# Weight operands of the MLP's first two pairs of chunks: made during the in-projection and loaded later

## The chip, the cores and the metric

The kernel runs on one core of a Trainium2 chip. The metric is the device time of one execution in microseconds (us); the kernel before takes 1713.9 us, the median of three executions (1712.73 to 1714.35). Engines: PE is TensorE (PEld its weight loads), DVE is VectorE, ACT is ScalarE, POOL is GpSimd, and SP is the engine whose queue issues nearly all transfers.

## The reference

One encoder layer over two groups of tokens (1024 and 256, together 1280) of width 1024, in fp32, with the same weights. Cut to what matters here:

```python
n = _rms_norm(h, g_mix, NORM_EPS)
z = jnp.einsum('bsd,dc->bsc', n, w_in).astype(f32)        # in-projection, 2304 columns
qa, ka, va, qb, kb, vb = jnp.split(z, cuts, axis=-1)
# mixer A: differential attention, 4 heads; mixer B: grouped-query attention with rotary positions
mixed = jnp.concatenate([oa, ob], axis=-1).astype(h.dtype)
h = h + jnp.einsum('bsc,cd->bsd', mixed, w_out)            # out-projection
n2 = _rms_norm(h, g_mlp, NORM_EPS)
a = jax.nn.relu(jnp.einsum('bsd,df->bsf', n2, w_ff1))      # MLP, 4096 columns
h = h + jnp.einsum('bsf,fd->bsd', a * a, w_ff2)
# then a gated per-layer embedding, and a final RMSNorm of h
```

The gain `g_mlp` of the norm is a factor on the rows of `w_ff1`. It depends on inputs alone, and so do all operands that are made from `w_ff1`; the products with them need `n2`, which is there only after the attention and the out-projection.

## The kernel before

**Numbers.** Every fp32 operand is split into a high part (type fp32r, by a copy on ScalarE) and a low part (operand minus high part, on VectorE or POOL). A product is three matmuls: high by high, high by low and low by high.

**Stages, by the trace.** In-projection to about 190 us; attention from then to about 720 us, with the rest of the in-projection and the out-projection woven in; a transition at 700 to 800 us, in which the last rows of the out-projection, the second norm, the transposes of the normed rows and the first products of the MLP run beside each other; first MLP product to about 1164 us; second to about 1530 us; then the gate, the embedding and the final norm.

**In-projection.** The pieces `b_unit` (queries, keys and values of mixer B, with norm and rotary positions), `va_unit` (values of mixer A) and `qk_a` (queries and keys of mixer A) are Python generators that yield after some matmuls. `weave` draws from two of them in turn. A tile of `b_unit` or `va_unit` is 24 matmuls of 128 x 256 into one PSUM bank (`psb`, `psv`, two banks each), which ScalarE (L283, L367) and then VectorE (L284, L368) read. Weights come by `load_w`: raw halves (`rawp`, `rawa`) are loaded, copied by ScalarE (L175) and subtracted (L176). `load` chains transfers of inputs: each is issued after the one before it in program order.

**First MLP product.** The 4096 columns are 32 chunks of 128, taken as 16 pairs (`NP1`). A pair is one step of a Strassen-Winograd scheme: 7 products instead of 8, each of a sum of quarters of the activations by a sum of quarters of the weights, in the order `O1` = 1, 6, 7, 2, 5, 4, 3. For each pair `w1_load` loads two raw blocks of 512 KB and multiplies them by the gain on POOL (eight pieces, L1012). `w1_ops` makes four sums (L1093, L1094, L1103, L1104) and seven splits (high L1087 on ScalarE, low L1088). For pairs 0 and 1 (`GS`) sums and all splits' low parts are on VectorE, for later pairs the sums and two of the low parts on POOL. The operands live in slots `W0` to `W11`; four of these, in rotation, take raw blocks. The activations' operands are split in `n_split` (high `nhi` L1120, low `nlo` L1121), from sums (`mlp_sums`, L1056) of transposed blocks (`trn`, copied by ScalarE in L1032 to `nb`); some pieces of them wait in `nlo` after a transfer that POOL issues (L1039). The first pair's products are made in two parts, 384 and then 256 columns of tokens, since the last two rows are normed last.

**What sets the order.** Each engine runs its own list of instructions in order. The lists are set when the kernel is built, by a scheduler that respects dependences and the orders that the program writes out (`issue_after`, `behind_norm`). In the transition the loop over `side` decides after how many finished rows of the out-projection (`op_done`) the loads of raw blocks and the first split are placed.

## Time and profile before

| what | value |
|---|---|
| median of three executions | 1713.9 us (1712.73 to 1714.35) |
| profiled execution: its time | 1711.62 us |
| profiled execution: its span | 1709.8 us |
| mean granted clock of TensorE | 0.997 |
| PE busy | 1668.8 us, 98% of the span |
| VectorE busy | 1183.8 us, 69% |
| ScalarE busy | 862.6 us, 50% |
| POOL busy | 686.2 us, 40% |

The span goes from the first to the last instruction of the profiled execution; the difference to its own time lies around it. The profile has a page with busy times per engine and per group of instructions, and the trace behind it gives the waits of an engine with what ended them, the timeline, and busy time by stretch with the clock that TensorE was granted.

### The profile page before, as it was taken

The numbers are of one execution on the slowest core, as the hardware profiler recorded it, in microseconds if no ns is written. First come the engines' busy times: TensorE is split into PE (matmuls) and PEld (weight loads), VectorE is DVE, ScalarE is ACT, GpSimd is POOL, SyncE is SP. The second block draws the span as 40 slices with busy tenths as digits, with TensorE's granted clock in tenths as the row PEclk, the third lists the DMA queues.
The fourth block names the chain that finished last, engine by engine and source line by source line (L and its number), as shares of the span: only waits on it lengthen the run. The fifth ranks groups of instructions, "written<-read, shape, count | busy, mean of one in ns | idle before, by whom it ended". The sixth has DMA issues, their size and how long they took to land.

```text
span 1709.8 us, 27198 instructions
## 1 busy us (share of the span) xinstructions
PE 1668.8 (98%) x9849; PEld 1488.8 (87%) x9849; DVE 1183.8 (69%) x2115; ACT 862.6 (50%) x1733; POOL 686.2 (40%) x667
## 2 busy tenths in 40 slices
PE   8999999999999999989999999999999999999997
PEld 8999889888788888879999999998888888888886
DVE  7866588787888878589775666666554865445666
ACT  8522377677766667684333333333333333354644
POOL 1224455555743444536565655520533400001441
PEclk9999999999999999999999999999999999999999
DMA  9923764433953623472443344359666465532111
GB/s 316 267 91 114 202 170 124 139 90 104 268 161 112 168 81 111 149 221 104 158 150 123 125 154 134 130 201 362 205 218 203 125 201 189 171 119 70 42 44 50
DMA packets 187835, 263.60 MB, mean 154 GB/s; under 512 B 13226, under 2 KB 120628, under 8 KB 187700
## 3 DMA queue, kind: packets, MB, share of 16 engines
q1 hardware_dynamic: 185956, 256.60, 47.4%
q0 software_dynamic: 1600, 5.24, 1.0%
q8 instruction: 78, 1.28, 0.3%
q14 instruction: 57, 0.47, 0.1%
q10 hardware_dynamic: 144, 0.00, 0.0%
HBM read 175.29 MB, written 81.27 MB: 150 GB/s over the span
## 4 chain that ended last, share of the span: by engine, by line
PE 76%; DVE 9%; ACT 4%; issue 4%; DMA 3%; POOL 3%; SPq 1%; POOLq 0%; DVEq 0%; ACTq 0%
PE psa L240 6%; PE sc L573 6%; PE av L651 5%; PE tr L627 4%; PE pso L240 4%; PE psb L240 3%; PE psv L240 2%; PE psg L1497 2%; DVE pl L638 1%; DVE nlo L1121 1%; DMA xt<-in_x 1%; DMA xr<-in_xT 1%; PE f__16240 L156 1%; PE f__15200 L156 1%; PE f__16582 L156 1%
## 5 line engine op out<-in xcount | busy, mean ns | idle before, releaser
L1299 ACT ACTIVATE ao<-ar 128x1280 fp32r<-128x1280 f32 x56 | 71.3, 1275 | 193.4 <-PE f__16244 L156 37.9
L573 PE MATMUL sc<-kt,qt 128*128 128x512 f32 (+1 forms) x576 | 156.7, 392 | 7.6 <-ACT p L598 4.8
L638 DVE TENSOR_TENSOR pl<-tr,ph 128x512 fp32r<-128x512 f32 x204 | 137.9, 684 | 31.2 <-ACT ph L633 29.9
L1301 DVE TENSOR_TENSOR ao<-ar,ao 128x1280 fp32r<-128x1280 f32 x56 | 88.8, 1587 | 100.1 <-ACT ao L1299 100.1
L633 ACT ACTIVATE ph<-tr 128x512 fp32r<-128x512 f32 x204 | 119.8, 595 | 58.0 <-PE tr L627 51.6
L1012 POOL TENSOR_SCALAR w1r<-w1r,gmlp 128x256 f32<-128x256 f32 x128 | 99.9, 797 | 66.3 <-DMA w1r<-in_w_ff 44.2
L240 PE MATMUL pso<-ow,mt 128*128 128x512 f32 x480 | 119.8, 396 | 3.1 <-DVE osq L678 1.3
L627 PE MATMUL tr<-ident,p 128*128 128x128 f32 x768 | 116.1, 274 | 6.3 <-DVE pl L638 5.5
L573 PEld LDWEIGHTS sc<-kt,qt 128*128 128x128 f32 x576 | 99.1, 189 | 25.8 <-ACT p L598 6.3
L1497 PE MATMUL psg<-gw,n 128*128 128x512 f32 (+1 forms) x504 | 115.4, 384 | 0.0
L627 PEld LDWEIGHTS tr<-ident,p 128*128 128x128 f32 x768 | 91.7, 141 | 23.2 <-DVE pl L638 9.5
L1497 PEld LDWEIGHTS psg<-gw,n 128*128 128x128 f32 x504 | 90.8, 188 | 19.5
L1087 ACT ACTIVATE w<-w1s 128x512 fp32r<-128x512 f32 x64 | 40.0, 628 | 133.1 <-POOL w1s L1094 64.0
L240 PEld LDWEIGHTS pso<-ow,mt 128*128 128x128 f32 x480 | 87.7, 189 | 21.1 <-DVE osq L678 2.0
L651 PE MATMUL av<-ph,vt 128*128 128x256 f32 x544 | 102.3, 289 | 1.0 <-ACT ph L633 0.4
L612 POOL TENSOR_SCALAR p<-p,rl 128x1024 f32<-128x1024 f32 x64 | 76.0, 1188 | 51.2 <-DVE rl L610 47.9
L590 DVE TENSOR_REDUCE mm<-sc 128x1 f32<-128x1024 f32 (+1 forms) x80 | 84.2, 1055 | 9.5 <-PE sc L573 9.1
L651 PE MATMUL av<-pl,vt 128*128 128x256 f32 x408 | 89.9, 302 | 0.0
L651 PEld LDWEIGHTS av<-ph,vt 128*128 128x128 f32 x544 | 82.3, 190 | 6.2 <-DVE osq L678 0.8
L598 ACT ACTIVATE p<-sc,mm 128x1024 f32<-128x1024 f32 x64 | 71.3, 1114 | 25.3 <-DVE mm L590 18.6
L586 DVE CUSTOM_DVE_ANT_0 p<-sc,dist 128x1024 f32<-128x1024 f32 x64 | 77.6, 1218 | 8.0 <-PE sc L573 4.4
L595 ACT ACTIVATE p<-p,mm 128x1024 f32<-128x1024 f32 x64 | 73.5, 1149 | 18.4 <-DVE mm L586 17.6
(1515 smaller groups left out, 4725.7 us busy)
## 6 DMA issues: line engine op xcount, KB each, us to landing
ar<-ad SPq DMA_DIRECT2D x56, 640.0 KB, 4.2
w2r<-in_w_ff SPq DMA_DIRECT2D x56, 512.0 KB, 4.5
qt<-qd SPq DMA_DIRECT2D x160, 128.0 KB, 3.0
ad<-q SPq DMA_DIRECT2D x64, 320.0 KB, 3.1
w1r<-in_w_ff SPq DMA_DIRECT2D x32, 512.0 KB, 4.4
ad<-qs SPq DMA_DIRECT2D x48, 320.0 KB, 2.2
md<-ml SPq DMA_DIRECT2D x40, 256.0 KB, 2.2
mt<-md SPq DMA_DIRECT2D x20, 512.0 KB, 6.0
```

What stands on the lines that cost most here:

```text
L240: PE.matmul(ps, a, b, start=i == 0, stop=i == n - 1)
L573: PE.matmul(ps[:, h0:h0 + n], shared["q"][:, cc, v, i * P:(i + 1) * P], kt[:, s0 + h0:s0 + h0 + n], start=v == 0, stop=v == 1)
L586: V.tensor_tensor_reduce(out=p[:, :sn], in0=ps[:, :sn], in1=dst_t[:, off:off + sn], scale=SLOPES[idx], scalar=3.0e38, op0=ALU.add, op1=ALU ...
L590: V.tensor_reduce(out=st["m", i][:, 0:1], in_=ps[:, :sn], axis=AX.X, op=ALU.max, negate=True)
L612: G.tensor_scalar(p[:, :sn], p[:, :sn], rl[:, 0:1], 1.0, op0=ALU.mult, op1=ALU.mult)
L627: PE.transpose(t[:, jj, i * P:(i + 1) * P], st["ws"][i][:, j * P:(j + 1) * P], ident)
L633: S.activation(ph, st["tr", j2], AF.Copy)
L638: V.tensor_tensor(pl, st["tr", j2], f(st["ph", j2][:]), op=ALU.subtract)
L651: PE.matmul(st["av"][:, :256], x_, y_, start=j2 == 0 and n == 0, stop=j2 == nj - 1 and n == len(pr) - 1)
L1012: G.tensor_scalar(raw[:, k], raw[:, k], gmlp[:, 4 * kh + k:4 * kh + k + 1], 1.0, op0=ALU.mult, op1=ALU.mult)
L1301: V.tensor_tensor(ao[:, 1], a, f(ao[:, 0]), op=ALU.subtract)
L1497: ends[:] = [PE.matmul(ps, a, b, start=m == 0, stop=m == len(pr) - 1)]
```

## The change

A new generator `early_w1` makes all seven operands of pairs 0 and 1 in the in-projection. For each pair it loads the two raw blocks into the slots `Q0` and `Q1`, multiplies them by the gain on ScalarE (eight pieces of 128 x 256), makes the four sums on POOL and the seven splits on ScalarE and VectorE, and stores each operand (512 KB, high and low part) to DRAM (`wed`). Its outputs share a two-buffer tile (`xt`) that the in-projection's statistics used before. `along` takes one step of it after every fourth yield of `b_unit(0)` and then of `b_unit(1)`: 16 steps in all.

In the transition `w1_fetch` loads a finished operand from `wed` straight into its slot: operand 1 of pair 0 when the first row of the out-projection is done, 6, 7, 2 and 5 after rows 4, 5, 6 and 8 (`FETCH`), 4 and 3 and the first three of pair 1 behind the last norm, the others of pair 1 during the second unit. The loads of raw blocks, the scalings on POOL, the sums and the splits of pairs 0 and 1 are gone from there. Raw blocks of pair 2, formerly loaded behind the last norm, and those of pair 3 are loaded in the second unit. The rotation of the slots for raw blocks and the slots of operands 1 and 5 are others, and two slots of the second MLP product (`KTS`) change places with them.

```diff
+    EVERY = 4
+    FETCH = ((4, 6), (5, 7), (6, 2), (8, 5))
...
-    weave(b_unit(0, w_b0), va_unit(1, w_va1), 1.0)
-    weave(b_unit(1, wload(1792, dma=load)), qk_a(0), 1.0)
+    NEW = 2
+    wed = {(p, i): dp.tile([P, 2, 4, P], F32, name=f"wed{p}_{i}") for p in range(NEW) for i in range(1, 8)}
+
+    def early_w1():
+        for p in range(NEW):
+            raws = []
+            for kh in range(2):
+                raw = slot(f"Q{kh}", [P, 4, 256], F32, "w1e")
+                load(raw, w_ff1[kh * 512:kh * 512 + 512, p * 256:(p + 1) * 256].rearrange("(k p) c -> p k c", p=P))
+                for k in range(4):
+                    S.activation(raw[:, k], raw[:, k], AF.Copy, scale=gmlp[:, 4 * kh + k:4 * kh + k + 1])
+                raws.append(raw)
+            a11, a12, a21, a22 = (raws[x][:, :, c * P:c * P + P] for c in range(2) for x in range(2))
+            yield
+
+            def out(i, src):
+                hl = bp.tile([P, 2, 4, P], F32R, tag="xt", name="w1o", bufs=2)
+                S.activation(hl[:, 0], src, AF.Copy)
+                V.tensor_tensor(hl[:, 1], src, f(hl[:, 0]), op=ALU.subtract)
+                dma(wed[p, i], f(hl[:]))
+
+            out(1, a11)
+            t = bp.tile([P, 2, 4, P], F32, tag="qkl", name="w1t", bufs=1)
+            s3, s2 = t[:, 0], t[:, 1]
+            G.tensor_tensor(s3, a11, a21, op=ALU.subtract)
+            G.tensor_tensor(s2, a22, s3, op=ALU.subtract)
+            yield
+            for i, src in ((6, s2), (7, s3), (2, a12)):
+                out(i, src)
+                yield
+            G.tensor_tensor(s3, a12, s2, op=ALU.subtract)
+            G.tensor_tensor(s2, a21, a22, op=ALU.add)
+            for i, src in ((5, s2), (4, a22), (3, s3)):
+                out(i, src)
+                yield
+
+    def along(main, side, every):
+
+        for n, c in enumerate(main):
+            yield c
+            if n % every == every - 1:
+                next(side, None)
+
+    early = early_w1()
+    weave(along(b_unit(0, w_b0), early, EVERY), va_unit(1, w_va1), 1.0)
+    weave(along(b_unit(1, wload(1792, dma=load)), early, EVERY), qk_a(0), 1.0)
+    drain(early)
...
+    WN = collections.defaultdict(dict)
+    EARLY = ({1: 3, 6: 10, 7: 9, 2: 11, 5: 8, 4: 1, 3: 4}, {1: 0, 6: 6, 7: 7, 5: 3, 4: 1, 2: 4, 3: 5})
+
+    def w1_fetch(p, i):
+        hl = slot(f"W{EARLY[p][i]}", [P, 2, 4, P], F32R, "w1")
+        dma(f(hl[:]), wed[p, i])
+        WN[p][i] = hl[:, 0], hl[:, 1]
...
+            if op_done and not WN[0]:
+                w1_fetch(0, 1)
...
-        raw = slot(("W8", "W9", "W10", "W11")[next(w1_n) % 4], [P, 4, 256], F32, "w1r")
+        raw = slot(("W10", "W9", "W11", "W8")[next(w1_n) % 4], [P, 4, 256], F32, "w1r")
...
-    WSLOT = {1: 3, 6: 6, 7: 7, 5: 0, 4: 1, 2: 4, 3: 5}
-    WN = {}
+    WSLOT = {1: 0, 6: 6, 7: 7, 5: 3, 4: 1, 2: 4, 3: 5}
...
-        if len(op_done) >= 6 and ops0 is None:
-            for kh in range(2):
-                w1_load(0, kh)
-            ops0 = w1_ops(0)
-            next(ops0)
-        if len(op_done) >= 8 and 1 not in w1raw:
-            for kh in range(2):
-                w1_load(1, kh)
+        for m, i in FETCH:
+            if len(op_done) >= m and i not in WN[0]:
+                w1_fetch(0, i)
...
-    for _ in range(2):
-        next(ops0)
-    behind_norm(lambda: drain(ops0))
+    w1_fetch(0, 4)
+    w1_fetch(0, 3)
+    for i in O1[:3]:
+        w1_fetch(1, i)
...
-    for kh in range(2):
-        w1_load(2, kh)
...
-    KTS = ("W3", "W6", "W7", "W0", "W1", "W4", "W5", "W2")
+    KTS = ("W0", "W6", "W7", "W3", "W1", "W4", "W5", "W2")
...
-        ops = w1_ops(u.p + 1) if n and u.p + 1 < NP1 else None
+        ops = w1_ops(u.p + 1) if n > 1 and u.p + 1 < NP1 else None
...
-            if ops and n == 1:
-                with tc.issue_after(splits[0].ins), tc.issue_after(splits[1].ins):
-                    next(ops, None)
-            elif ops:
+            if ops:
                 next(ops, None)
+            elif n == 1:
+
+                if i in (5, 4, 3):
+                    w1_fetch(1, {5: 5, 4: 4, 3: 3}[i])
+                if i == 3:
+                    w1_fetch(1, 2)
+                if i in (6, 7, 2, 5):
+                    w1_load(2 if i in (6, 7) else 3, int(i in (7, 5)))
```

**How the order moves.** TensorE at the end of the out-projection, before (`pso` are the last out-projection products, `trn` transposes, `f1` the MLP's products; the number after `nhi`, `nlo` or `w1` tells the operand):

```order
L240 MATMUL pso_10174<-ow_7158,mt_10131 128x512
...
L156 MATMUL f1__10318<-nhi1_9825,w1_9912 128x384 x4
L156 MATMUL f1__10318<-nlo1_9663,w1_9912 128x384 x2
L1024 MATMUL trn_10153<-ident_82,h_sb_6220 128x128 x4
...
L156 MATMUL f1__10333<-nhi6_9954,w1_10248 128x384 x8
L156 MATMUL f1__10333<-nlo6_9668,w1_10248 128x384 x4
L156 MATMUL f1__10347<-nhi7_10100,w1_10251 128x384
L1024 MATMUL trn_10220<-ident_82,hn_10139 128x128 x4
...
L156 MATMUL f1__10347<-nhi7_10100,w1_10251 128x384 x7
L156 MATMUL f1__10347<-nlo7_9669,w1_10251 128x384 x4
L156 MATMUL f1__10395<-nhi4_10211,w1_10262 128x384
L1024 MATMUL trn_10234<-ident_82,hn_10190 128x128 x4
```

and in the changed kernel:

```order
L242 MATMUL pso_10258<-ow_7262,mt_10215 128x512
...
L156 MATMUL f1__10380<-nlo1_9769,w1_9214 128x384 x4
L1083 MATMUL trn_10237<-ident_82,h_sb_6324 128x128 x4
...
L156 MATMUL f1__10395<-nhi6_10048,w1_9858 128x384 x8
L156 MATMUL f1__10395<-nlo6_9774,w1_9858 128x384 x4
L156 MATMUL f1__10409<-nhi7_10184,w1_9946 128x384 x8
L156 MATMUL f1__10409<-nlo7_9775,w1_9946 128x384 x4
L1083 MATMUL trn_10304<-ident_82,hn_10223 128x128 x4
...
L156 MATMUL f1__10457<-nhi4_10295,w1_10332 128x384 x8
L1083 MATMUL trn_10318<-ident_82,hn_10274 128x128 x4
```

The transposes of the last row but one stand behind product 7 now, and those of the last row behind eight matmuls of product 4 instead of one. Four matmuls of product 1 are left behind the last `pso` where there were eight; the other four are in front.

ScalarE around the high parts of products 2 and 4, before (`nst` are the norm's small pieces):

```order
L1206 ACTIVATE q<-f__10318 128x384
L922 ACTIVATE hn,nst<-h_sb 128x512
L924 ACTIVATE nst<-nst 128x1
L926 ACTIVATE nst<-nst 128x1
L1087 ACTIVATE w_10254<-w1r 128x512
L1087 ACTIVATE w_10262<-w1r 128x512
L1120 ACTIVATE nhi_10268<-nlo_9664 128x4x384
L1120 ACTIVATE nhi_10211<-nlo_9666 128x4x384
L1032 ACTIVATE nb<-trn 128x512
```

and in the changed kernel:

```order
L1258 ACTIVATE q<-f__10380 128x384
L1091 ACTIVATE nb<-trn 128x512 x2
L979 ACTIVATE hn,nst<-h_sb 128x512
L981 ACTIVATE nst<-nst 128x1
L983 ACTIVATE nst<-nst 128x1
L1177 ACTIVATE nhi_10342<-nlo_9770 128x4x384
L1177 ACTIVATE nhi_10295<-nlo_9772 128x4x384
L1177 ACTIVATE nhi_10184<-nt 128x4x128
```

The two copies of weights ahead of the high parts are gone; the high parts follow the last row's norm directly.

ScalarE at the start of the weave of `b_unit(0)` and `va_unit(1)`, before (`whp` is a split of the in-projection's weights, `vl` the values' high part):

```order
L367 ACTIVATE vl<-psv,rstd_95 128x2x128
L139 ACTIVATE rq2u<-rq2v 128x2
L140 ACTIVATE rr<-rq2u 128x2
L175 ACTIVATE whp<-rawp 128x512
L433 ACTIVATE lam_e<-lam_e 128x2
L175 ACTIVATE whp<-rawp 128x512 x2
```

and in the changed kernel (`w1e` is a raw block of the MLP's weights, `w1o` an operand's buffer):

```order
L369 ACTIVATE vl<-psv,rstd_95 128x2x128
L459 ACTIVATE w1e<-w1e,gmlp 128x256
L139 ACTIVATE rq2u<-rq2v 128x2
L459 ACTIVATE w1e<-w1e,gmlp 128x256 x3
L177 ACTIVATE whp<-rawp 128x512
L435 ACTIVATE lam_e<-lam_e 128x2
L140 ACTIVATE rr<-rq2u 128x2
L459 ACTIVATE w1e<-w1e,gmlp 128x256 x4
L466 ACTIVATE w1o<-w1e 128x512
```

The last split of `va_unit(1)`'s weights now stands behind four scalings, and these behind the transfer of the raw block. The two splits that followed it belong to `b_unit(1)` and are made later.

More of the change, by code (lines that the diff above doesn't have):

```diff
@@ L1080, in w1_ops @@
         a11, a12, a21, a22 = r0[:, :, 0:P], r1[:, :, 0:P], r0[:, :, P:], r1[:, :, P:]
-        ws = WN[p] = {}
-        GS = G if p > 1 else V
+        ws = WN[p]
         def split(i, src, eng=V):
@@ L1092, in w1_ops @@
         s3, s2 = t[:, 0], t[:, 1]
-        GS.tensor_tensor(s3, a11, a21, op=ALU.subtract)
-        GS.tensor_tensor(s2, a22, s3, op=ALU.subtract)
+        G.tensor_tensor(s3, a11, a21, op=ALU.subtract)
+        G.tensor_tensor(s2, a22, s3, op=ALU.subtract)
         yield
@@ L1099, in w1_ops @@
         yield
-        split(2, a12, GS)
+        split(2, a12, G)
         yield
-        GS.tensor_tensor(s3, a12, s2, op=ALU.subtract)
-        GS.tensor_tensor(s2, a21, a22, op=ALU.add)
+        G.tensor_tensor(s3, a12, s2, op=ALU.subtract)
+        G.tensor_tensor(s2, a21, a22, op=ALU.add)
         split(5, s2)
         yield
-        split(4, a22, GS)
+        split(4, a22, G)
         yield
         split(3, s3)
-        if 0 < p < NP1 - 2:
+        if p < NP1 - 2:
             for kh in range(2):
@@ L1123, in encoder_kernel @@
     splits = []
-    trs, steps, ops0 = transposes(), 0, None
+    trs, steps = transposes(), 0
     w1raw = {}
```

## The prediction

> **What bounds the kernel now.** I began with the page's busy times, then went through the span in stretches, then to the waits of TensorE in the one stretch that is not full.
>
> ```profile
> span 1709.8 us, 27198 instructions
> PE 1668.8 (98%) x9849; PEld 1488.8 (87%) x9849; DVE 1183.8 (69%) x2115; ACT 862.6 (50%) x1733; POOL 686.2 (40%) x667
> ```
>
> TensorE works through 98% of the span, so work taken from another engine is worth only the TensorE idle time that it causes. Where the change acts, this is stretch by stretch (columns: length, busy time of PE, PEld, DVE, ACT and POOL, granted clock, DMA share, GB/s):
>
> ```profile
> 740.00:750.00 10.00, 8.87 (x49) 7.47 (x48) 8.49 (x23) 6.67 (x15) 6.07 (x9) 1.00 1.03 328
> 750.00:760.00 10.00, 10.00 (x57) 8.90 (x56) 8.56 (x16) 8.09 (x17) 1.53 (x3) 1.00 0.54 177
> 760.00:770.00 10.00, 6.84 (x33) 6.04 (x32) 10.00 (x17) 9.90 (x18) 0.71 (x1) 0.84 0.17 57
> 770.00:780.00 10.00, 9.02 (x58) 8.76 (x57) 10.00 (x15) 7.25 (x10) 5.27 (x1) 0.99 0.33 107
> 780.00:790.00 10.00, 7.79 (x59) 7.21 (x58) 10.00 (x18) 4.11 (x8) 10.00 (x8) 1.00 0.00 0
> 790.00:800.00 10.00, 10.00 (x67) 10.00 (x66) 8.84 (x18) 5.28 (x12) 2.09 (x4) 1.00 0.40 121
> ```
>
> This is the transition from the out-projection to the MLP. PE's idle time in it is 1.13 + 3.16 + 0.98 + 2.21 = 7.5 us, while VectorE is full from 760 to 790. Below full speed, the clock costs at most 0.16 x 10 + 0.01 x 10 = 1.7 us more. The waits of PE from 735 to 800 name the producers:
>
> ```profile
> PE f__10395 L156 <- ACT nhi L1120: 2.8, 1, 2.8
> PE pso L240 <- DMA mt<-md: 1.1, 1, 1.1
> PE f__10449 L156 <- DVE nlo L1121: 1.1, 1, 1.1
> PE f__10379 L156 <- DVE w L1088: 1.0, 1, 1.0
> PE f__10502 L156 <- ACT nhi L1120: 0.8, 1, 0.8
> PE trn L1024 <- ACT nb L1032: 0.3, 1, 0.3
> PE f__10524 L156 <- DVE q L1213: 0.3, 1, 0.3
> ```
>
> They sum to 7.4 us. Only one of them, 1.0, is a wait for a weight operand; the others are for activations (nhi, nlo), a transfer and small pieces. So the stake is 7.4 + 1.7 = 9.1 us, and the question is how much the engines that stay on the path owe to the weight work that goes.
>
> **The change part by part.**
>
> *The longest wait.* The timeline from 757 on shows what stood in ScalarE's queue ahead of it (columns: start, length):
>
> ```profile
> 757.96 0.64 ACT L1120 ACTIVATE nhi<-nlo 128x512 fp32r<-128x512 f32 x1 [0.86 <-DMA nlo<-nb]
> ...
> 758.50 1.06 ACT L1032 ACTIVATE nb<-trn 128x512 f32<-128x512 f32 x2
> ...
> 759.82 0.64 ACT L922 ACTIVATE hn<-h_sb 128x512 f32<-128x512 f32 x1
> ...
> 761.02 1.14 ACT L1087 ACTIVATE w<-w1r 128x512 fp32r<-128x512 f32 x2
> ...
> 761.33 0.85 PE L156 MATMUL f__10347<-nlo,w 128*128 128x384 f32 x4
> ...
> 762.06 2.84 ACT L1120 ACTIVATE nhi<-nlo 128x1536 fp32r<-128x1536 f32 x2
> ...
> 764.96 0.44 PE L156 MATMUL f__10395<-nhi,w 128*128 128x384 f32 x1 [2.77 <-ACT nhi L1120]
> ```
>
> PE is done with product 7 near 762.2 and stops until the second of two pieces of 1.42 us (nhi of product 2, then of product 4) ends at 764.9. Directly ahead of the two stand the copies of weights (L1087), 762.06 - 761.02 = 1.04 us, which the change removes. The copy at 756 goes too, but it lies ahead of a wait for a transfer (0.86, the first row) and gives nothing unless that transfer lands sooner. So nhi of product 4 comes at least 1.04 us earlier; with some 0.7 from the shorter queue before 758 it is ready at 763.1. In the changed order PE still comes to it at about 762.0, since only the places of the transposes and of product 1's rest moved. Remainder: 1.1 us, of 2.8 (bounds: 0, or 1.8 where only the 1.04 comes off).
>
> *VectorE's share.* These groups of 735 to 800 are the weight work:
>
> ```profile
> L1012 POOL TENSOR_SCALAR w1r<-w1r,gmlp 128x256 f32<-128x256 f32 x18 | 22.5, 1266 | 22.0 <-DVE nt L1056 14.0 <-ACT q L1197 7.9
> ...
> L1088 DVE TENSOR_TENSOR w<-w1s,w 128x512 fp32r<-128x512 f32 x8 | 5.7, 707 | 0.0
> L1087 ACT ACTIVATE w<-w1s 128x512 fp32r<-128x512 f32 x8 | 5.0, 630 | 6.6 <-PE f__10466 L156 3.6 <-DVE w1s L1094 1.0 <-PE f__10502 L156 0.8
> L1088 DVE TENSOR_TENSOR w<-w1r,w 128x512 fp32r<-128x512 f32 x7 | 5.0, 715 | 0.0
> ...
> L1087 ACT ACTIVATE w<-w1r 128x512 fp32r<-128x512 f32 x7 | 4.2, 619 | 0.0
> ...
> L1093 DVE TENSOR_TENSOR w1s<-w1r 128x512 f32<-128x512 f32 x2 | 1.5, 742 | 0.1
> ```
>
> VectorE made 15 low parts (10.7 us) and 8 sums (four such groups of two, about 5.7 us) here; ScalarE 15 copies (9.2 us). About 17 of the VectorE pieces, some 10 us, fall in its full stretch 757 to 797, so it gets down to about three quarters. The wait for nlo (1.1) then shrinks to about 0.2, and the one for w (1.0) is gone. ScalarE however keeps a run of nhi pieces for the second half's columns, each about 0.6 us, in one queue with the transposes' copies: for the 0.8 + 0.3 + 0.3 of the last rows of the waits I take three like waits of 0.3, 0.6 and 0.7 (bounds: 0, or the 1.4 that stands there and 0.8 more).
>
> *The transfers in the transition.* Until 760, four operands of 512 KB are loaded where four raw blocks of 512 KB were; so the wait for mt stays between 0 and 1.1, and I take 0.6. Behind the last norm five more are issued at about 755.5, and product 4's and 3's slots are only free then. By the 6.2 us that such a load of raw weights took here (the row below), product 4's, the third of the five, lands at 761.7, just ahead of nhi. It is what is late next if it takes over 763.1 - 755.5 = 7.6 us.
>
> ```profile
> w1r<-in_w_ff SPq DMA_DIRECT2D x2, 512.0 KB, 6.2
> ```
>
> *The clock.* A remainder of 1.1 us instead of 2.8 would keep most of it: I take 0.5 of the 1.7 as still lost (0 to 1.7). The rows show 0.84 around the one gap of 2.77 us and 1.00 in the stretch with 1.13 us idle. By the Trainium skill, "TensorE: Matmul & The Clock Gate" (Part 1, What's actually happening), the clock halves after an idle window of about 3.4 us, and these windows run freely; by that rule a gap of 1.1 us costs no clock at all, the whole 1.7 would return and the gain be 0.5 us more, an estimate from that page. The trace agrees in part: here a gap shorter than the window was enough.
>
> Sum for the transition: left over are 1.1 + 0.2 + 1.6 + 0.6 + 0.5 = 4.0, so 9.1 - 4.0 = 5.1 us come back.
>
> *What the in-projection takes on.* Added there are 16 scalings, 14 copies and 14 subtractions, 8 sums, 2 MB of loads and 7 MB of stores.
>
> ```profile
> 66.00:123.00 57.00, 56.88 (x486) 56.68 (x486) 40.95 (x119) 18.89 (x51) 17.08 (x21) 1.00 0.49 151
> ...
> 123.00:185.00 62.00, 62.00 (x428) 57.03 (x428) 43.43 (x117) 18.61 (x50) 25.97 (x30) 1.00 0.28 98
> ```
>
> ScalarE gets 14 x 0.63 (L1087) + 16 x 0.47 (its 128x256 piece below) = 16 us on 18.9, VectorE 14 x 0.71 (L1088) = 10 on 41, POOL 8 x 1.29 (the group below) = 10 on 17. Were all of it in the first 57 us, they would stand at 0.62, 0.89 and 0.48. The DMA's 9.4 MB are 29 us at the 328 GB/s of 740 to 750, spread over 119 us at shares of 0.49 and 0.28. Nothing is full, so what counts is order: a piece that waits holds the tile behind it. How long PE bears that, one tile shows:
>
> ```profile
> L176 POOL TENSOR_TENSOR wla<-rawa,wha 128x512 fp32r<-128x512 f32 x3 | 3.8, 1290 | 7.3 <-ACT wha L175 7.3
> ```
>
> ```profile
> 95.28 0.47 ACT L367 ACTIVATE vl<-psv,rstd 128x256 fp32r<-128x256 f32 x1 [0.23 <-PE psv L240]
> ...
> 96.66 0.47 DVE L368 SCALAR_TENSOR_TENSOR vl<-psv,rstd,vl 128x256 fp32r<-128x256 f32 x1
> ```
>
> A psv bank is full at 95.05 and read out by 97.13; a tile is 48 matmuls of 57 / 486 = 0.117 us, 5.6 us, and with two banks this one is wanted again at 100.7. So 3.6 us are spare in each tile, against about 0.63 + 0.71 us of added work. The scalings wait for their loads, first at 65 us, where the transfers are busiest; behind the first four stands ScalarE's last split of V's weights (L175, formerly at 65.78), whose products begin about 70, the first tile's last quarter. The load is issued where this stands now, at 61.6:
>
> ```profile
> 61.59 0.89 SPq L93 DMA_DIRECT2D rawp<-in_w_in  x2
> ```
>
> ```profile
> rawp<-in_w_in SPq DMA_DIRECT2D x12, 256.0 KB, 4.2
> ...
> xt<-in_x SPq DMA_DIRECT2D x2, 512.0 KB, 6.8
> ```
>
> Both rows are of 40 to 80 us. With 4.2 us it lands at 65.8 and all is in time; with 6.8, the other load of 512 KB, at 68.4, four scalings of 0.47 end at 70.3 and the split at 70.9, 0.9 us late. I take 0.4, between them (0 to 3: the 0.9 once, and twice more for the two loads of pair 1). The loads of the next weights (rawp, rawa), passed on SP's queue by those of pair 1, still come some 20 us ahead of use. POOL's sums stand ahead of the rotary additions, whose results have a tile to spare.
>
> *The late rotation of slots.* One load of the second MLP weight is moved some 20 us later, into 1150 to 1180, where the transfers are full:
>
> ```profile
> 1150.00:1180.00 30.00, 30.00 (x166) 26.97 (x165) 22.01 (x28) 13.65 (x17) 2.41 (x1) 1.00 1.04 395
> ```
>
> PE is full as well, and uses those operands 10 us or more after they are made; 512 KB more at 395 GB/s are 1.3 us. I take 0; without that cover it would be 1.3.
>
> Total: 5.1 - 0.4 = 4.7 us. The profiled execution took 1711.6 us (1709.8 of span), so 1706.9 by it; the median is 1713.9, and I put the same difference there: **1709.2 us**.
>
> **The rivals.**
>
> *Nearly all comes back.* If the shorter queues let every nhi and nlo be early, all 9.1 us return: 1713.9 - 9.1 = 1704.8. For it: VectorE and ScalarE are the named producers of six of the seven waits. Against it: the two nhi pieces of 1.42 us stay in a row, behind the last norm's ScalarE pieces (759.82 to 761.0), which end when the last row of the out-projection ends.
>
> *The last row's chain sets the pace.* The wait for nhi at 757.96 is for a transfer, the norm hangs on the last h_sb; neither is touched. Then only the 1.04 and the 1.0 come back, 2.0 us, less 0.4: 1712.3, or nothing if fetched operands for products 4 and 3 are late by as much. For it: the 2.8 is a sum of untouched pieces but for 1.04.
>
> *Slower: the in-projection's queues.* Each store of an operand holds one of two buffers; ScalarE's copy for the next but one waits for it, and in its queue stand the reads of PE's banks. It decides once a hold passes the 3.6 us. At 0.7 us past it for each of 14 operands PE loses 9.8, net 9.8 - 5.1 = 4.7 slower: 1718.6. For it: no engine could pass a held piece. Against: operands follow each other by about a tile of 5.6 us, and the large stores of this stretch land in less:
>
> ```profile
> kd<-qkl SPq DMA_DIRECT2D x2, 512.0 KB, 3.7
> ```
>
> That the work does not leave the transition is excluded: the order of the changed kernel has no weight piece there.
>
> **How the numbers follow.** The forecast gets 0.47, with its own range 1706.5 to 1711.5; nearly all 0.18; the last row's chain 0.25; slower 0.10. About 0.2% (3.4 us) is the least that a measurement of this kernel can tell from no change. Faster than 1710.5 are nearly all and 0.42 of the forecast's 0.47: 0.60. Within 0.2%: 0.25 + 0.05 = 0.30. Slower: 0.10. The range for 8 in 10 goes from 1704.8, all back, to 1714.0, the chain with a late fetch; left out is mainly the slower case.
>
> **What would show it.** In the changed profile: no weight piece (L1087, L1088 of before) on VectorE or ScalarE from 735 to 795; VectorE at 0.7 to 0.8 there; first wait of product 4 about 1 us, still for ScalarE's nhi; clock 0.95 or more in its stretch of 10 us; PE idle from 740 to 790 near 3.5 us. PE full from 66 to 185, within 0.5 us. I am wrong if product 4 waits for a transfer into w, if the wait on nhi stays above 2 us, or if PE waits for vl, sq or whp in the in-projection for more than 1 us.

## The result, and the profile after

The changed kernel takes 1717.69 us (median of seven executions, 1717.17 to 1720.6) and the kernel before 1712.73 us (median of seven, 1710.3 to 1714.35): a ratio of 1.0032, with a 95% interval of 1.0020 to 1.0044. The ratio is not the quotient of the two medians: by it the change is slower by about 5.5 us, by the medians by 5.0, where 4.7 us faster was forecast; 1717.69 is outside the range. The profiled execution of the changed kernel is its slowest one, 1720.6 us with a span of 1718.7, so its trace shows some 3 us more than the median does.

The transition first. The waits of TensorE from 735 to 830 us in the changed kernel (what waited, for whom, us in total, times, longest):

```profile
PE f__10426 L156 <- ACT nb L1091: 0.9, 1, 0.9
PE f__10457 L156 <- ACT nhi L1177: 0.9, 1, 0.9
PE f__10592 L156 <- DVE q L1265: 0.6, 1, 0.6
PE trn L1083 <- ACT nb L1091: 0.4, 1, 0.4
```

and its busy time by stretch (columns as in the prediction):

```profile
740.00:750.00 10.00, 10.00 (x54) 8.48 (x53) 6.05 (x16) 7.13 (x18) 3.13 (x5) 1.00 1.04 355
750.00:760.00 10.00, 10.00 (x55) 8.65 (x54) 6.82 (x18) 7.84 (x19) 5.91 (x9) 1.00 1.00 308
760.00:770.00 10.00, 10.00 (x50) 8.36 (x49) 6.76 (x15) 7.78 (x16) 2.19 (x3) 1.00 1.05 338
770.00:780.00 10.00, 8.69 (x55) 8.05 (x54) 8.71 (x19) 8.00 (x15) 0.75 (x1) 1.00 0.87 299
780.00:790.00 10.00, 9.05 (x59) 8.61 (x60) 10.00 (x13) 7.93 (x13) 0.00 (x0) 1.00 0.35 107
790.00:800.00 10.00, 9.44 (x69) 9.27 (x68) 10.00 (x18) 3.68 (x7) 4.11 (x6) 1.00 0.52 157
```

The longest wait, for nhi of product 4, fell from 2.8 to 0.9 us; those for nlo, for a weight operand and for mt are gone; the clock is full. So in this trace the transition did what was forecast. The loss is far ahead of it. The waits of TensorE from 60 to 190 us, where the kernel before had one of 0.6:

```profile
PE trb L325 <- DVE ro L303: 7.6, 2, 6.2
PE psb L242 <- DVE vbl L350: 2.6, 1, 2.6
PE psb L242 <- DVE zg L286: 1.3, 1, 1.3
```

and busy time there, in the changed kernel:

```profile
66.00:100.00 34.00, 31.48 (x256) 31.39 (x257) 22.23 (x64) 13.20 (x37) 10.76 (x12) 0.95 0.56 197
100.00:130.00 30.00, 21.06 (x161) 20.42 (x161) 24.38 (x58) 15.98 (x41) 14.76 (x16) 0.89 0.88 292
130.00:160.00 30.00, 30.00 (x217) 28.07 (x216) 22.64 (x64) 9.22 (x25) 10.33 (x12) 1.00 0.53 188
```

TensorE idles 2.5 + 8.9 = 11.5 us there, and the clock below 1.00 costs up to 0.05 x 34 + 0.11 x 30 = 5.0 us more. VectorE is busy for 0.81 of the worst stretch, ScalarE for 0.53 and POOL for 0.49: no engine is full, yet TensorE waits for the rotary result (ro). The timeline of the changed kernel shows where it begins (columns: start, length, what ended the idle time before):

```profile
80.48 0.37 SPq L320 DMA_DIRECT2D kd<-qkl  x1
...
82.19 0.74 POOL L294 TENSOR_TENSOR ra<-zg,cs 128x256 f32<-128x256 f32 x1 [3.63 <-DVE zg L286]
86.69 1.31 POOL L473 TENSOR_TENSOR w1t<-w1e 128x512 f32<-128x512 f32 x1 [3.76 <-DMA vad<-vl]
87.96 0.74 POOL L301 TENSOR_TENSOR ra<-ra,rb 128x256 f32<-128x256 f32 x1
...
88.73 1.52 DVE L303 TENSOR_TENSOR ro<-ra,rr 128x256 f32<-128x256 f32 x1 [3.71 <-POOL ra L301]
...
90.00 1.16 ACT L466 ACTIVATE w1o<-w1t 128x512 fp32r<-128x512 f32 x2 [5.78 <-POOL w1t L474]
91.06 0.46 ACT L285 ACTIVATE sq<-psb,rstd 128x256 f32<-128x256 f32 x1
```

The first sum (w1t, L473) lies in the one buffer of the key and value unit's output (`tag="qkl"`, one buffer). The last store from it (kd) is issued at 80.48 and takes 6.1 us by the list of transfers, so it lands at 86.6, and the sum starts at 86.69. (The trace names the last transfer that ended nearby, vad; the time fits kd, and two runs below decide it.) Behind the sum POOL's rotary addition waits, behind that VectorE's ro; ScalarE waits 5.8 us for the sum, and behind it the read of a full bank (sq). TensorE does not stop here yet. It does when the second pair comes. The waits of ScalarE from 60 to 160 us:

```profile
ACT rq4u L139 <- DVE rq4v L138: 21.3, 10, 6.1
...
ACT w1e L459 <- DMA w1e<-in_w_ff: 7.5, 3, 2.7
ACT w1o L466 <- POOL w1t L474: 5.8, 1, 5.8
...
ACT w1o L466 <- DMA wed<-w1o: 2.4, 1, 2.4
```

Three times it stands still for a raw block (7.5 us), once for a store of an operand (2.4), and each time the reads of TensorE's banks stand behind. What was held is done from 111 to 126 us all at once, when VectorE works 13.8 of 15 us; TensorE waits 6.17 us of these for one rotary result.

### The profile page after: what moved, and what is told of

It reads as the page before. It is cut to its first block, busy times and chain, and to the rows that moved or that the text cites. A ratio compares the mean times of both kernels' runs of the same rounds, so it can differ in the third digit from the quotient of the medians.

```text
span 1718.7 us, 27284 instructions
## 1 busy us (share of the span) xinstructions
PE 1669.3 (97%) x9849; PEld 1490.0 (87%) x9849; DVE 1183.8 (69%) x2107; ACT 868.4 (51%) x1749; POOL 673.4 (39%) x659
## 4 chain that ended last, share of the span: by engine, by line
PE 76%; DVE 8%; DMA 6%; ACT 4%; issue 3%; POOL 2%; SPq 1%; POOLq 0%; ACTq 0%; DVEq 0%
PE psa L242 6%; PE pso L242 5%; PE sc L621 5%; PE av L699 5%; PE tr L675 4%; PE psb L242 2%; PE psg L1553 2%; DMA vad<-vl 1%; DVE pl L686 1%; DMA xt<-in_x 1%; PE psv L242 1%; PE f__16296 L156 1%; PE f__15256 L156 1%; PE f__16638 L156 1%; PE f__15601 L156 1%
## 5 line engine op out<-in xcount | busy, mean ns | idle before, releaser
L1352 DVE TENSOR_TENSOR ao<-ar,ao 128x1280 fp32r<-128x1280 f32 x56 | 93.3, 1666 | 89.0 <-ACT ao L1350 89.0
L1071 POOL TENSOR_SCALAR w1r<-w1r,gmlp 128x256 f32<-128x256 f32 x112 | 79.2, 726 | 69.1 <-DMA w1r<-in_w_ff 48.3
L1144 ACT ACTIVATE w<-w1s 128x512 fp32r<-128x512 f32 x56 | 35.2, 628 | 116.4 <-POOL w1s L1151 54.4
```

The lines of the kernel that those rows point to most:

```text
L1071: G.tensor_scalar(raw[:, k], raw[:, k], gmlp[:, 4 * kh + k:4 * kh + k + 1], 1.0, op0=ALU.mult, op1=ALU.mult)
L1352: V.tensor_tensor(ao[:, 1], a, f(ao[:, 0]), op=ALU.subtract)
```

## The experiments

Each kernel was timed beside the kernel before on the same chip; the ratios are to that, with 95% intervals, and can differ by up to 0.0007 from the quotient of the medians. Differences in us between two experiments are worked out from their ratios.

### The in-projection alone

The kernel before with the early operands made and stored, and never loaded:

```diff
-    weave(b_unit(0, w_b0), va_unit(1, w_va1), 1.0)
-    weave(b_unit(1, wload(1792, dma=load)), qk_a(0), 1.0)
+    early = early_w1()          # as in the change, with wed and along
+    weave(along(b_unit(0, w_b0), early, EVERY), va_unit(1, w_va1), 1.0)
+    weave(along(b_unit(1, wload(1792, dma=load)), early, EVERY), qk_a(0), 1.0)
+    drain(early)
```

> The kernel before with the early operands made and stored as in the change, but never loaded; the transition is that of before. Theory A: the loss of the in-projection stands alone: 11 to 15 us slower than before, 1724 to 1728, with the same waits of TensorE on ro, zg and vbl. Theory C (the loss in the changed kernel's trace is chance or comes from elsewhere): less than 5 us slower.

Measured: 1725.18 us, 1.0071 (1.0056 to 1.0086), about 12.2 us slower. The waits of TensorE from 60 to 190:

```profile
PE trb L324 <- DVE ro L302: 8.0, 2, 6.2
PE psb L241 <- DVE vbl L349: 1.1, 1, 1.1
PE psb L241 <- DVE zg L285: 1.0, 1, 1.0
```

The same waits with the same longest one: the loss belongs to the making and storing of the operands, and is there without anything that the change does later. Theory A's number holds; whether the queues or the stores' transfers cost it, this run does not tell. POOL's first sum waits here too, and this trace names kd:

```profile
82.96 1.31 POOL L471 TENSOR_TENSOR w1t<-w1e 128x512 f32<-128x512 f32 x1 [3.39 <-DMA kd<-qkl]
```

### The transition alone

First try: a stored column block of the split activations in place of each operand, at the same 14 steps.

```diff
-            out(i, src)          # and all that makes src
+            dma(wed[p, i].rearrange("a v k c -> a (v k c)"), f(xh[:, i, 0:1024]))
```

> Leaves out the making of the 14 operands: at the same 14 steps of the in-projection a column block of the split activations is stored in their place, 512 KB each, and fetched later as in the change, so the products of pairs 0 and 1 are not the reference's. Theory A (the changed kernel loses its 5 us in the in-projection, by pieces that wait in ScalarE's, POOL's and VectorE's queues, and gains in the transition what was forecast): TensorE idles at most 1 us from 66 to 160 us, its idle time from 740 to 800 stays at the changed kernel's 2.8 us, and the median is 5 to 7 us below before, 1706 to 1708. Theory B (the transfers of the stores themselves hold the in-projection up): idle time from 66 to 160 stays above 5 us and the median is at or above before.

Measured: 1720.32 us, 1.0042 (1.0027 to 1.0057), against theory A's number; TensorE idles 8.0 us from 66 to 160, so by the letter this is theory B's result. Its trace shows 740 to 800 as in the change (56.78 us busy of 60), but TensorE loses time earlier than the change did: nothing in these stores waits for the tiles, so all 14 were issued from 40 to 69 us, where the transfers are nearly full already (0.95 and 0.99 of the DMA's time from 50 to 70). The longest of its waits from 60 to 190 us:

```profile
PE rp L441 <- DVE vbl L350: 5.9, 1, 5.9
```

This kernel tells that transfers moved into that stretch cost much by themselves, and nothing about theory B in the change's own places. So a second try stores one block and loads it 14 times:

```diff
-        dma(f(hl[:]), wed[p, i])
+        dma(f(hl[:]), wed[0, 1])
```

> Leaves out the making of the operands: one block of the split activations is stored once in the in-projection and loaded in place of each of the 14 operands, so the products of pairs 0 and 1 are not the reference's. The transition is that of the change. Theory A (the transition returns what was forecast; all loss is in the in-projection): TensorE idles at most 1.2 us from 66 to 160 us and 2.5 to 4.5 us from 740 to 800; the median is 5 to 7 us below before, 1706 to 1708. Theory E (the transition's gain is lost again later or was never there): within 2 us of before.

Measured: 1706.68 us, 0.9972 (0.9961 to 0.9982), about 4.8 us faster, just short of theory A's 5 to 7 and far from theory E; the forecast for the transition was 5.1. In its profile (span 1709.3 us) the idle time is above the expected in both places: 2.9 us from 66 to 160 (at most 1.2 expected) and 4.7 from 740 to 800 (2.5 to 4.5). Since 13 of the 14 stores are gone too, theory B falls only with the ordered kernels below, which make all of them. Loss and gain alone add up to 12.2 - 4.8 = 7.4 us; the change measured 5.5, within the two intervals.

### The buffer of the sums

```diff
-            t = bp.tile([P, 2, 4, P], F32, tag="qkl", name="w1t", bufs=1)
-            s3, s2 = t[:, 0], t[:, 1]
+            s3, s2 = (bp.tile([P, 4, P], F32, tag="raw", name="w1t", bufs=RAWB) for _ in range(2))
```

> The changed kernel, with the two sums of a pair in two buffers of the raw in-projection weights instead of the buffer that the key and value unit's last store (kd) still reads. Theory A1 (the first sum on POOL waits until 86.7 us for that store, and what is late behind it piles up later): the sum starts by 77, TensorE's waits on ro from 100 to 130 shrink from 7.6 us to under 4, and the time falls by 3 to 8 us against the changed kernel, to 1710 to 1715. Theory A2 (only the second pair's loads and VectorE's load from 105 to 126 count): no change beyond 1 us, 1717 to 1718.

Measured: 1713.55 us, 1.0008 (0.9999 to 1.0017). POOL's first sum, and TensorE's waits from 60 to 190:

```profile
66.65 1.30 POOL L472 TENSOR_TENSOR w1t<-w1e 128x512 f32<-128x512 f32 x1 [2.24 <-ACT w1e L459]
```

```profile
PE trb L325 <- DVE ro L303: 3.0, 2, 2.8
PE psv L242 <- DVE vl L370: 0.6, 1, 0.6
```

The sum starts 20 us earlier and the waits on ro fall from 7.6 to 3.0: theory A1, and the kd store it was. From 1.0032 to 1.0008 is about 4 us of the 12 that the in-projection lost.

### Loads ahead of the scalings

The same, with the raw blocks of both pairs loaded in the first two steps (pair 0 into `zl`'s two buffers, pair 1 into `Q0` and `Q1`):

```diff
+                raw = (slot(f"Q{kh}", [P, 4, 256], F32, "w1e") if p else
+                       zp.tile([P, 4, 256], F32, tag="zl", name="w1e"))
+                load(raw, ...)
+            yield
+        for p in range(NEW):     # the scalings, sums and splits, as before
```

> As the previous kernel, and the raw blocks of both pairs are loaded at the first two steps, a step or more ahead of their scalings (pair 0 in the two buffers of the query and key unit's output, pair 1 in the two slots). Theory A2: ScalarE no longer waits 7.5 us for loads, the waits of TensorE from 66 to 160 fall from 11.5 us to under 4, and the time is 1707 to 1711. Theory D (VectorE's added work, and its pieces that stand still while POOL works, are the cause): the waits on ro from 105 to 126 stay above 5 us and the time above 1714.

Measured: 1713.33 us, 1.0003 (0.9993 to 1.0012): not told from the last kernel. ScalarE's wait for the blocks fell to 1.4 us, but TensorE now waits 4.5 us on ro and 1.3 on vbl, all ahead of 92 us. With the loads gone from the queue the work bunches earlier instead of at 105 to 126. Neither theory came out: the loads were not what mattered, and the waits left the place that theory D named.

### The sums on VectorE

```diff
-            G.tensor_tensor(s3, a11, a21, op=ALU.subtract)
+            V.tensor_tensor(s3, a11, a21, op=ALU.subtract)     # and the other three
```

> The changed kernel with the sums' own buffers (the third experiment), and the eight early sums on VectorE instead of POOL. Theory F (pieces of VectorE stand still while POOL runs a two-operand piece of 1.3 us, and this delays ro): TensorE's waits on ro from 100 to 120 fall from 3.0 to under 1 us, and the time falls by 2 to 4 us against the third experiment, to 1709.5 to 1711.5. Theory G (VectorE's amount of work in this stretch is the cause, and the sums add 5.4 us to it): the waits grow and the time rises by 1 to 4 us, to 1714.5 to 1717.5.

Measured: 1713.25 us, 1.0003 (0.9989 to 1.0017), where the buffer's kernel had 1.0008. No difference that can be told; neither theory F nor G is supported, though the two could have cancelled.

### Spreading the steps

A step's VectorE pieces are put behind the rotary result of the tile before it, and the second query unit's weights are made ahead. `issue_after` orders within one engine's list, so only VectorE's pieces are bound, which the expectation's "each step" does not say. The sums keep their own buffers.

```diff
+                with tc.issue_after(anchor[0].ins):     # anchor: the last ro
                     next(side, None)
...
+    w_b1 = wload(1792, dma=load)
     weave(along(b_unit(0, w_b0), early, EVERY), va_unit(1, w_va1), 1.0)
```

> The changed kernel with the sums' own buffers; besides, each step of the early work is bound to come after the rotary result of the tile before it, so that one operand falls to one tile, and the second query unit's weights are loaded and split ahead of the early work, as in the kernel before. All the early work is still done, on the same engines. Theory H (the work fits; what costs is that it is bunched and stands ahead of the tiles' own pieces): TensorE idles under 1.5 us from 66 to 190, and the time is 1706.5 to 1709, below before by 0.2% or more. Theory G (the amount of work): idle time of 3 us or more, 1710 or above.

Measured: 1711.35 us, 0.9995 (0.9985 to 1.0005). By the letter this is theory G's result (idle time of 3 us or more, 1710 or above) and not H's; the ordered kernels below speak against G. A wait on ro of 3.3 us near 125 is left. In this kernel's timeline, ScalarE holds the read of a bank (sq, 116.27) behind an operand's copy that waited for a store and four scalings that waited for their block:

```profile
112.60 0.63 ACT L468 ACTIVATE w1o<-w1e 128x512 fp32r<-128x512 f32 x1 [1.30 <-DMA wed<-w1o]
114.13 1.71 ACT L461 ACTIVATE w1e<-w1e,gmlp 128x256 f32<-128x256 f32 x4 [0.90 <-DMA w1e<-in_w_ff]
115.75 0.62 ACT L177 ACTIVATE wha<-rawa 128x512 fp32r<-128x512 f32 x1
116.27 0.46 ACT L287 ACTIVATE sq<-psb,rstd 128x256 f32<-128x256 f32 x1
```

That this hold, two tiles earlier, makes the wait near 125 is a reading of the trace; the kernels with the order on every engine test it together with the other lists.

The same with the sums on VectorE:

> As the previous kernel, with the early sums on VectorE. Theory H: within 1 us of the previous kernel, since each tile has spare time for either. Theory F alone: lower than the previous kernel by 2 us or more. Theory G: higher than it by 2 us or more.

Measured: 1710.24 us, 0.9991 (0.9981 to 1.0001), again no difference to the last that can be told. And the spread kernel with the sums in the shared buffer:

> The changed kernel with its steps spread as in the spread kernel (each after the tile before it, second query unit's weights ahead), but with the sums on POOL in the buffer that the key unit's store reads, as the change has it. If the buffer costs by bunching what is behind the sum (theory A1), the spread makes it harmless: within 1.5 us of the spread kernel, 1710 to 1713. If the hold of POOL's queue itself costs, 1714 to 1717.

Measured: 1715.6 us, 1.0014 (1.0005 to 1.0024), some 3 us above the spread kernel: the shared buffer, which holds POOL's queue, costs by itself, with this spread or without.

### A wrong lead: lambda

The change's profile shows 2.6 us of waiting for vbl at 66 us, with VectorE held by lambda's load. In three kernels the whole of lambda's work was moved behind the first weave: in the spread kernel with sums on VectorE, in the kernel before, and in the change.

```diff
+    weave(...)                 # first weave
     lam_t = bp.tile(...)       # from here to neglam, formerly ahead of it
```

> The spread kernel with the sums on VectorE, and the load and small pieces of lambda placed after the first weave (all work is done, on the same engines). Theory I (what the spread kernel still loses, 3.6 us against the transition alone, lies at 65 to 70 us, where VectorE holds a read of a full bank behind lambda's load): TensorE no longer waits for vbl beyond 0.6 us, the clock stays at 1.00 from 66 to 100, and the time falls by 1.5 to 3.5 us to 1707 to 1709, below before by more than its uncertainty. Theory J (the rest is the amount of added work all along the in-projection): no change beyond 1 us, 1709.5 to 1711.

> The kernel before with lambda placed after the first weave: the control for the last. The wait there is 0.6 us in the profile of before, so 0 to 1.5 us faster than before; where it is as much faster as the spread kernel, the early work has no part in that wait.

> The changed kernel, with lambda placed after the first weave and nothing else. By theory I the wait on vbl of 2.6 us and the slow clock from 65 to 75 (1.7 us) go: 1713 to 1715 against the changed kernel's 1717.7. By theory J less than 1 us: 1717 to 1718.

Measured: 1712.28 us, 0.9995 (0.9986 to 1.0003); 1712.32 us, 0.9999 (0.9990 to 1.0008); 1718.11 us, 1.0028 (1.0017 to 1.0038). None differs from its model beyond the intervals. The wait for vbl is gone in all three and the time is not: theory I falls. In the change with lambda later the waits on ro are 7.8 us and all waits of TensorE from 60 to 190 are 8.7, against 7.6 and 11.5 in the change's profile. Whether that difference is one of the kernels, one profile of each does not tell.

### The order on every engine

Now each step's pieces stand behind the last piece of the tile before on all four lists that they use:

```diff
+                with ExitStack() as order:
+                    for a in anchor:       # ro (VectorE), sq (ScalarE), ra (POOL), vad's store (SP)
+                        order.enter_context(tc.issue_after(a.ins))
+                    next(side, None)
```

Three kernels: with loads ahead and the sums on VectorE, with loads ahead and the sums on POOL, and with the loads where the change has them and the sums on VectorE.

> The early work as in the spread kernel with sums on VectorE, but every engine (ScalarE, VectorE, POOL and the transfers, not VectorE alone) takes a step's pieces behind its own last piece of the tile before; and each pair's raw blocks are loaded a step or more ahead of their scalings, pair 0 in the query and key unit's two output buffers, pair 1 in the two slots. Theory K (the spread kernel's last loss is ScalarE, held by the second pair's load and by a store ahead of the read of a bank): TensorE's wait on ro near 125 us (3.3 to 4.4 us in three spread kernels) goes, idle time from 66 to 190 under 1 us, 1706 to 1709, below before beyond its uncertainty. Theory J (the amount of added work): 1710 to 1712.

> As the previous kernel, with the sums on POOL as in the change. By theory K within 1 us of the previous kernel; where VectorE's pieces that stand still while POOL works count, 1 to 3 us above it.

> As the first of these three, but both pairs' raw blocks are loaded into the two slots, as in the change, so that the second pair's loads wait for the first pair's last quarter and its scalings for the loads. Theory K: ScalarE again waits 1 us or more for the second pair's blocks and TensorE loses 1 to 4 us near 125, 1708 to 1711. If ordering alone removes the loss: as the first.

Measured: 1707.49 us, 0.9975 (0.9965 to 0.9985); 1708.49 us, 0.9979 (0.9970 to 0.9988); 1707.52 us, 0.9975 (0.9966 to 0.9983). All three beat both kernels, by 3.6 to 4.3 us against before. The third differs from the spread kernel with the sums on VectorE (0.9991) by the order on the other three lists alone, which took about 2.7 us; the rest of the loss had gone with the sums' own buffers and with the spread and its earlier weights. The second is 0.7 us above the first, less than can be told. The first and the third are alike: theory K's load as the cause is not supported, though in the third ScalarE does wait for blocks as K said, and TensorE loses 1.9 us, 0.8 of it at 138 and none near 125. Theories J and G fall, since all the added work is still done, and theory B, since all 14 stores are. Waits of ScalarE from 66 to 190 us in the third kernel:

```profile
ACT w1e L461 <- DMA w1e<-in_w_ff: 4.2, 3, 2.4
ACT w1o L468 <- DMA wed<-w1o: 3.8, 4, 2.1
```

It still stands for blocks and stores 8.0 us in all, against 9.9 in the change, and 9.3 for the sums against 5.8. Busy time in the same kernel:

```profile
66.00:100.00 34.00, 32.94 (x277) 32.56 (x278) 25.83 (x78) 15.34 (x41) 7.79 (x11) 1.00 0.60 204
100.00:130.00 30.00, 30.00 (x254) 29.77 (x253) 21.39 (x58) 14.90 (x39) 8.89 (x12) 1.00 0.57 192
130.00:160.00 30.00, 29.18 (x199) 26.45 (x198) 27.06 (x69) 10.81 (x28) 12.02 (x14) 1.00 0.64 226
```

TensorE loses 1.9 us here instead of 11.5, and the clock is full. VectorE works 74 us in the three stretches, against 69 in the change. By these runs, what decides is not how long a piece waits nor how much is added, but which piece stands behind it: here, one whose tile has its whole spare time left. The last half of this is argued from the order as written, not measured. Against the transition alone (0.9972), what the added work still costs is 0.5 us by the third kernel, less than can be told.

What stays open: how the loss beside the shared buffer splits up among ScalarE's, POOL's and the transfers' lists. The spread on VectorE with earlier weights took about 2 (0.9995 against 1.0008), the order on the other three some 2.7 more (0.9979 against 0.9995 with the sums on POOL, 0.9975 against 0.9991 with them on VectorE); no run binds one of these alone, or has the earlier weights without the spread. One candidate was not tried at all: more than two buffers for the operands. ScalarE's waits for their stores, 2.4 us in the change, are 7.9 in the buffer's kernel, 10.9 in the spread kernel and 3.8 in the third ordered one (66 to 190 us).

## Why the prediction was wrong

**The transition was right in its mechanism.** Forecast: 5.1 us back; the transition alone measured 4.8. Left over were to be 1.1 (nhi of product 4), 0.2 (nlo), 1.6 (three small ones), 0.6 (mt) and 0.5 of clock. The trace of the change has 0.9, none, 1.9 (0.9 + 0.6 + 0.4), none, and none; TensorE idles 2.8 us from 740 to 800. No fetched operand was late, product 4's among them, and VectorE came down from 0.93 to 0.81 of the 60 us. Of the clock all came back: with no wait above 0.9 us the granted clock is 1.00 throughout. The Trainium skill, "TensorE: Matmul & The Clock Gate" (Part 1, What's actually happening), which has the clock halve after an idle window of about 3.4 us, agrees with this trace. The spread kernel does not agree with it, and there the measurement decides: waits of 1.5 and 1.1 us, close together, went with a clock of 0.83 (row in the last section). That the sum and the measurement lie so close is in part luck: by the rows of 740 to 800 the change's trace got back 9.1 - 2.8 = 6.3 us, that of the transition alone 9.1 - 4.7 = 4.4.

**The failed step is "What the in-projection takes on", 0.4 us with bounds 0 to 3.** It measured 12.2 alone (9.6 to 14.7 by its interval). Four things in it were wrong. It held the added work per tile, 0.63 + 0.71 us, against 3.6 us of spare time of a bank, as if a step fell on each tile; but the engines' lists put several steps together, behind pieces that wait. With each step bound to its tile on every list, and the sums in buffers of their own, the same work cost 0.5 us, so the sizes of the pieces were not the error. It looked at the bank and took one sentence for the rotary additions ("whose results have a tile to spare"); that was where TensorE waited, 7.6 of the 11.5 us. It did not follow the tag: the sums were written into a buffer whose last reader was a store in a busy stretch, about 4 us by the runs. And it put no loss of clock there, where the change's rows allow up to 5.0 us. The price for late loads (0.9 us each) was of the right kind for ScalarE, which waited 2.5 us a time; yet the kernel with ordered lists waits much the same and loses nothing that can be told.

**The slower rival** had the sign and nearly the size (4.7 us slower, measured 5.5), with a chance of 0.10. The size was luck: it came from 0.7 us assumed for each operand, with no row behind it. Its place was half right: in-order queues ahead of TensorE's reads, but in the change the store and its two buffers made 2.4 us of ScalarE's waits, against 7.5 for loads and 5.8 for POOL's sum, and TensorE waited mostly for ro, 7.6 us, not for the read of a bank, 3.9. The evidence for more than 0.10 stood in what the prediction quoted: VectorE at 0.89 if all went into the first weave, one buffer in the diff, and in the order scalings in front of a split that TensorE needs.

**The late rotation** was right: TensorE is full from 1150 to 1200 us in both traces.

## What to carry to other kernels

Work put beside a full TensorE is not priced by its mean share of each engine: follow each in-order list, and ask of every added piece what it waits for and which read of TensorE's stands behind it; a buffer's tag with its last reader is such a wait. Before giving up work that fits but costs, bind its pieces on every list to come right behind the last piece of the tile before: here that, with buffers of their own for the sums and the second query unit's weights made ahead, turned 0.32% slower into 0.25% faster with the same work. And measure the two halves of a move apart, the place that loses the work and the place that takes it: each was plain alone, and the sum told neither.

## What the runs showed of the hardware

**A small VectorE piece can be held until POOL's two-operand piece beside it ends.** Rows of the changed kernel's timeline, POOL and VectorE:

```profile
117.89 1.59 POOL L178 TENSOR_TENSOR wla<-rawa,wha 128x512 fp32r<-128x512 f32 x1 [1.99 <-ACT wha L177]
...
118.25 1.25 DVE L146 TENSOR_TENSOR rq4u<-rr 128x4 f32<-128x4 f32 x1
...
123.39 1.30 POOL L480 TENSOR_TENSOR w1t<-w1e 128x512 f32<-128x512 f32 x1
...
123.49 1.22 DVE L138 TENSOR_SCALAR rq4v<-ss 128x4 f32<-128x4 f32 x1
...
126.42 0.16 DVE L149 TENSOR_TENSOR rr<-rr,rq4u 128x4 f32<-128x4 f32 x1
```

A piece of 128 x 4 elements takes 0.16 us (last row) and here 1.25 and 1.22; both end within 0.1 us of POOL's piece (119.48 and 124.69). Not every piece is held: a reduction (L289) at 120.42, inside POOL's sum of 120.18 to 121.47, took 0.40 us. The Trainium skill, "GPSIMD Engine Reference" (1. Specifications), says that POOL shares its memory interfaces with VectorE, and that VectorE's instructions contend with it when they are in a 2-port perf mode or have two inputs in SBUF, the on-chip memory. The rows agree that some do, and give the length; whether the piece of L138, which has one input, ran in such a mode, no run here shows. No run shows that this cost anything in all: with the sums moved from POOL to VectorE nothing changed that can be told, in three pairs of kernels (1.0008 and 1.0003, 0.9995 and 0.9991, 0.9979 and 0.9975). But that also adds work to VectorE, so a gain and a loss may have cancelled, and the pair was not run with the shared buffer, where the wait of 6.17 us lies among pieces held like this.

**A wait of 2.6 us can slow the clock for 3.4 us, and one of 2.8 us can leave it full.** Matmuls of the changed kernel around the wait for vbl:

```profile
68.53 0.55 PE L242 MATMUL psb<-whp,xh 128*128 128x256 f32 x1 [2.59 <-DVE vbl L350]
...
71.53 0.41 PE L242 MATMUL psb<-whp,xh 128*128 128x256 f32 x1
71.74 0.35 PE L242 MATMUL psb<-wlp,xh 128*128 128x256 f32 x1
71.93 0.28 PE L242 MATMUL psb<-whp,xl 128*128 128x256 f32 x1
```

and its busy time and clock around the wait of 6.17 us:

```profile
120.00:125.00 5.00, 0.00 (x0) 0.00 (x0) 4.97 (x10) 0.22 (x2) 4.82 (x5) 0.81 0.85 287
125.00:130.00 5.00, 4.03 (x19) 4.03 (x20) 4.79 (x15) 2.78 (x8) 1.95 (x4) 0.51 0.83 210
130.00:135.00 5.00, 5.00 (x45) 5.00 (x44) 4.03 (x9) 1.19 (x3) 2.46 (x2) 1.00 0.79 282
```

After a wait of 2.59 us, matmuls took 0.35 us and more instead of 0.28 until 71.9, 3.4 us after the first; after 6.17 us the clock was 0.51 over five microseconds. In the change's profile the 11.5 us of waits thus had up to 5.0 us of clock behind them, somewhat under half as much again. But the length of one wait does not settle it. The buffer's kernel had a wait of 2.77 us, as long as the one that went with 0.84 in the kernel before, and its matmuls were back at 0.28 us 0.6 us later (granted clock 1.00 from 105 to 115):

```profile
109.90 0.44 PE L325 MATMUL trb<-ident,ro 128*128 128x128 f32 x2 [2.77 <-DVE ro L303]
...
110.53 0.28 PE L242 MATMUL psb<-wlp,xh 128*128 128x256 f32 x1
```

And in the spread kernel's transition two shorter waits, 1.5 and 1.1 us with 1.1 us of transposes between them, went with a clock of 0.83:

```profile
760.00:770.00 10.00, 7.34 (x38) 6.71 (x37) 7.48 (x15) 8.63 (x16) 0.75 (x1) 0.83 0.63 230
```

What decides between these, no run here shows.
